# Four rows of a forward substitution as one multiply-add with a column scalar each

## The chip, the cores and the metric

The kernel runs on one core of a Trainium2 chip. Its engines are TensorE (PE, matmuls; PEld is its weight load), VectorE (DVE), ScalarE (ACT), GpSimd (POOL) and SyncE (SP), which here only issues DMAs. The metric is the device time of one execution in microseconds; lower is better. Before the change it is 3082.83 us, the median of three runs (3080.05 to 3083.95).

## The reference

One layer of a hybrid decoder for one sequence of 2048 tokens and 8 short ones of 4, width 1024, 16 heads of 64. A normalised input goes through one wide projection; a short gated convolution and an RWKV-7 recurrence work on parts of it; gates merge the two, an output projection and a residual follow. The part in which the change lies is the recurrence:

```python
def step(S, inp):
    r_t, k_t, v_t, d_t, kk_t, a_t = inp
    sa = jnp.einsum('bhvk,bhk->bhv', S, -kk_t)
    S = (S * d_t[:, :, None, :] + sa[..., None] * (kk_t * a_t)[:, :, None, :]
         + v_t[..., None] * k_t[:, :, None, :])
    y = jnp.einsum('bhvk,bhk->bhv', S, r_t)
    return S, y
```

## The kernel before

**Stages.** The tokens are worked on in four sets of 512 (`th`), and within a set in eight pairs of heads (`p`). While a pair is worked on, TensorE runs projections of the wide matrix for the next pair: blocks of 24 matmuls (8 slices of the contraction, three products of split 32-bit values each), written `ip<-XH,whl` and `ip<-XL,whl` in the profile. `XH` and `XL` are the two parts of the set's input, `whl` the two parts of a weight. After the fourth set come the output projections (`acc`).

**A pair.** The recurrence is computed in chunks of 64 steps: keys (`rwkv_keys`), the solve (`rwkv_solve`), the merge (`rwkv_merge`), loads, the chain over the chunks (`rwkv_chain`: `pa`, `UB`, `pb`, `SV`, `S`), outputs (`rwkv_out`: `Yc`, `mu_`). Each is a generator that yields after a few operations; `drive` runs the projections and lets these side jobs in between.

**The solve.** For each chunk a triangular matrix has to be inverted. Its 32x32 diagonal blocks, two for each of two heads and eight chunks, 32 in all, are inverted by substitution on VectorE. A transpose puts the matrix into `Mi` and the identity into `X` such that a lane holds 8 columns of a block's inverse; then the loop of lines 1215 to 1222 goes over the rows from j = 31 to 1. Row j takes column j of `X` (the 8 - j // 4 column groups that can be other than zero there), multiplies it by row j of `Mi` and adds the product to the columns to the left. These are two operations: the product into `tt`, a buffer of two, and the addition into `X`. For j = 31 to 28 there is one group, number 7, so both have 31 to 28 elements per lane. The 62 operations of a pair depend on each other one by one. Behind them a transpose (`Mi<-X`) makes room for the merge, which runs copies on ScalarE (`Xbd`), transposes on VectorE (`Mc`) and small matmuls (`pt<-Mc`).

**What sets the order.** All engine calls go through one helper (line 264), so that nearly all of the profile's rows are of that line. It books each operation with an assumed cost on a clock of its own: on VectorE 145 ns and 1.05 ns per element, and 58 ns more for a multiply-add with a column scalar (lines 302 to 309). A side job may go on when its inputs are ready by that clock. When all is written down, the instructions of VectorE and ScalarE are put in order of their planned starts and held to it. The order on TensorE, GpSimd and SyncE is that in which the code was written down. So another cost in one operation can move all that follows.

**Splitting weights.** From the second set on, `comb` reads quarters of the output weights (`q`), combines them, and `part_of` splits each into two parts in one of two buffers `qs` by turns and hands a store to `SP.store`. This queue keeps up to two stores back until their data is ready by the planner's clock (lines 324 to 334).

Of the kernel before, what the change touches and what calls it, by code (L numbers as in the profile page):

```python
# [11 lines left out]
ALU = mybir.AluOpType  # L12
# [14 lines left out]
W = {"sq": 1.0, "norm": 1.0, "lora": 2.0, "one": 1.0, "scan": 2.0, "exp": 2.0, "key": 1.0, "bones": 1.5,  # L27
     "sv": 1.5, "bt": 2.0, "score": 4.0, "inv0": 5.0, "inv": 0.45, "inv1": 4.0, "merge": 2.0,
     "gk": 1.3, "us": 1.3, "sa": 1.3, "state": 1.3, "samp": 2.0, "gn": 4.0, "out": 2.0}
# [315 lines left out]
def hybrid_kernel(tc, x_prompt, x_sample, state_conv, state_shift, state_rwkv, norm_g, w_in, conv_w,  # L345
# [5 lines left out]
    V, A, G, T = (Traced(e, n, clock) for e, n in ((nc.vector, "DVE"), (nc.scalar, "ACT"), (nc.gpsimd, "POOL"), (nc.tensor, "PE")))  # L351
    SP = Queue(nc.sync, clock)
# [327 lines left out]
    for q in range(2):  # L680
        V.tensor_tensor(out=mask_s[:, q, 0:NSAMP].rearrange("p (j i) -> p j i", i=SL),
                        in0=mask_p[:, q, 0:NSAMP].rearrange("p (j i) -> p j i", i=SL),
                        in1=seqm.unsqueeze(2).broadcast_to([P, NS, SL]), op=ALU.mult)
# [493 lines left out]
    def rwkv_solve(th, p, o):  # L1177

        AR = o["AR"]
        samp = th == LAST  # L1180
        GM = GMB[(th * NB + p) % 2]


        yield 0.0, (), 2
        for c0 in range(0, NCH + samp, 4):
            cs = range(c0, min(NCH + samp, c0 + 4))
            pp = [new_pt([P, 512], F32, name="pt") for _ in range(2)]
            for c in cs:
                for h in range(2):
                    T.matmul(pp[h][:, (c - c0) * P:(c - c0 + 1) * P], lhsT=BK[HS[h], c].rearrange("p q t -> p (q t)"),  # L1190
                             rhs=AR[HS[h], c].rearrange("p q t -> p (q t)"), start=True, stop=True)
            k = len(cs)
            mk = mask_s if c0 == NCH else mask_p
            for h in range(2):
                V.tensor_tensor(out=GM[:, c0:c0 + k, :, h, :],
                                in0=pp[h][:, 0:k * P].rearrange("p (c a t) -> p c a t", a=2, t=64),
                                in1=mk.unsqueeze(1).broadcast_to([P, k, 2, 64]), op=ALU.mult)
            yield W["score"], (), 2 if c0 + 4 < NCH + samp else 0


        Mc = rw.tile([P, NCH, 32], F32, name="Mc")
        for i, g in enumerate(blk):
            h, b = i // 2, slice(i % 2 * 32, i % 2 * 32 + 32)
            A.copy(Mc[g], GM[b, 0:NCH, 0, h, b])
        yield 0.5, [Mc]
        Mi = rw.tile([P, 32, 32], F32, name="Mi")
        V.transpose(Mi.rearrange("p t (e c) -> p t e c", c=NCH),
                    Mc.rearrange("p c t -> p t c").unsqueeze(2).broadcast_to([P, 32, 4, NCH]))
        X = rw.tile([P, 8, 32], F32, name="X")
        A.copy(X, X0)  # L1210
        Mo = rw.tile([P, NCH, 32], F32, name="Mo")
        A.copy(Mo[64:96], GM[0:32, 0:NCH, 0, 1, 32:64])
        yield W["inv0"], [Mi, X]

        for j in range(31, 0, -1):
            c0 = j // 4
            tt = sm.tile([P, 80], F32, name="tt")
            tv = tt[:, 0:(8 - c0) * j].rearrange("p (c i) -> p c i", i=j)
            V.tensor_tensor(out=tv, in0=Mi[:, j, 0:j].unsqueeze(1).broadcast_to([P, 8 - c0, j]),
                            in1=X[:, c0:8, j:j + 1].broadcast_to([P, 8 - c0, j]), op=ALU.mult)  # L1220
            V.tensor_tensor(out=X[:, c0:8, 0:j], in0=X[:, c0:8, 0:j], in1=tv, op=ALU.add)
            yield W["inv"]
        Xo = rw.tile([P, 32, 32], F32, name="Mi")[:, 0:8].rearrange("p a (e c) -> p a e c", c=8)
        V.transpose(Xo.rearrange("p a e c -> p (a e c)"), X.rearrange("p a b -> p (a b)"))
        o.update(GM=GM, Xo=Xo, Mo=Mo)
        yield W["inv"]
# [333 lines left out]
    def part_of(w, key, j, src, scale=1.0):  # L1560

        hl = qs[turns[0] % 2]
        turns[0] += 1
        yield 1, [src]
        A.activation(out=hl[:, 0], in_=src, func=AF.Copy, scale=scale)
        yield 1, [hl[:, 0]]
        V.scalar_tensor_tensor(out=hl[:, 1], in0=src, scalar=scale, in1=hl[:, 0].bitcast(F32), op0=ALU.mult, op1=ALU.subtract)
        SP.store(units[w][key][j // 2][:, :, j % 2 * 4 * P:(j % 2 + 1) * 4 * P], hl.bitcast(F32))
# [4 lines left out]
    def comb():  # L1573

        add, sub = ALU.add, ALU.subtract
        for w, src in (("c", w_out_c[0]), ("r", w_out_r[0]), ("o", w_o[0])):
            for j in range(4):
# [9 lines left out]
                if w == "o":  # L1587
                    for q in ("11", "12", "21", "22"):
                        yield from part_of(w, q, j, qr[q], 0.5)
                    combined("11", "12", "11", sub)  # L1590
                    yield from part_of(w, "t1", j, qr["11"], 0.5)
                    combined("12", "22", "12", sub)
                    yield from part_of(w, "t3", j, qr["12"], 0.5)
                    combined("22", "22", "11", sub)
                    yield from part_of(w, "t2", j, qr["22"], 0.5)
                    combined("21", "21", "22", sub)
                    yield from part_of(w, "t4", j, qr["21"], 0.5)
                else:
                    for q in ("11", "12", "21", "22") if w == "c" else ("11", "12", "22"):
                        yield from part_of(w, q, j, qr[q])  # L1600
                    combined("22", "21", "22", add)
                    yield from part_of(w, "s1", j, qr["22"])
                    combined("21", "11", "21", sub)
                    yield from part_of(w, "s3", j, qr["21"])
                    combined("22", "22", "11", sub)
                    yield from part_of(w, "s2", j, qr["22"])
                    combined("12", "12", "22", sub)
                    yield from part_of(w, "s4", j, qr["12"])
# [119 lines left out]
    def begin_pair(th, p, total):  # L1728


        o = {}
        k = th * NB + p
        f = [total * x for x in CUTS["end" if end_(th, p) else "most" if th < LAST else "last"]]
        def read(n):
            return [prior(x, n) for x in ("chain", "samp")]
        job["keys", k] = Side(rwkv_keys(th, p, o), "keys", [prior("load", k - 1), prior("solve", k - 1), prior("up", 0)] + read(k - 2)).over(0, f[3])
        job["solve", k] = Side(rwkv_solve(th, p, o), "solve", [job["keys", k], prior("merge", k - 1)] + read(k - 2)).over(f[3], f[4])
        job["merge", k] = Side(rwkv_merge(th, p, o), "merge", [job["solve", k]] + read(k - 2)).over(f[4], f[5])
        job["load", k] = Side(rwkv_load(th, p, o), "load", [job["keys", k]] + read(k - 1)).over(f[4], f[5])
        return o  # L1740
# [389 lines left out]
```

## Time and profile before

| | us |
|---|---|
| median of three runs | 3082.83 |
| the profiled execution | 3081.61 |
| its span in the profile | 3079.9 |
| DVE, products `tt<-Mi,X`, 992 | 216.4 |
| DVE, additions `X<-X,tt`, 992 | 211.0 |

The profile is of one execution. Between its time and the span lie 1.7 us ahead of the first instruction and behind the last. The span is what the engines' rows are measured against. Products and additions of the substitution have 427.4 us together, a fifth of VectorE's busy time. In rows with an instruction, the columns are its start, its duration, the engine, and what it writes and reads; in brackets stands how long the engine was idle before it and what ended that. In grouped rows, the number behind x is the count, then busy time in us and the mean of one in ns. Idle time of an engine that isn't waited for costs nothing.

### The profile page before, as it was taken

What the parts mean: (1) busy time and instruction counts of PE and PEld (TensorE: products, weight loads), DVE (VectorE), ACT (ScalarE), POOL (GpSimd) and SP (SyncE); (2) the same over time, 40 slices, a digit from 0 to 9 for tenths busy, and PEclk for the clock granted to TensorE, in tenths of its full rate; (3) what the DMA queues carried; (4) which work ended last, traced back from release to release, by engine and by line L of the source; (5) the groups of instructions that cost most, each with busy time, mean ns of one, the idle gap of its engine ahead of it and who ended that gap; (6) DMA issues with size and microseconds to landing.
All of it is one profiled execution on the core that took longest, in us unless ns stands there. A gap on an engine that the chain in (4) does not pass through costs nothing. (4 is left out here: it accounts for less than half of the span.)

```text
span 3079.9 us, 56086 instructions
## 1 busy us (share of the span) xinstructions
PE 3004.7 (98%) x21418; PEld 2574.5 (84%) x21418; DVE 2140.3 (69%) x5606; ACT 1338.9 (43%) x2691; POOL 311.2 (10%) x520
## 2 busy tenths in 40 slices
PE   7999999999999999899999999999999999999998
PEld 6777877788878788788888889999999999888996
DVE  5777767766777777777766666666676774486575
ACT  5455555544444444444444444444444442224223
POOL 2011111111111110111111111000000000000000
PEclk9999999999999999999999999999999999999999
DMA  7877767656767676766644444444334447987775
GB/s 270 274 241 239 236 210 255 228 193 222 243 222 235 230 241 218 238 225 239 223 169 155 169 152 151 141 148 144 130 129 144 140 156 239 352 332 291 281 261 193
DMA packets 293937, 659.15 MB, mean 214 GB/s; under 512 B 46394, under 2 KB 162227, under 8 KB 242982
## 3 DMA queue, kind: packets, MB, share of 16 engines
q1 hardware_dynamic: 293670, 655.58, 62.4%
q8 instruction: 169, 2.77, 0.3%
q14 instruction: 98, 0.80, 0.1%
HBM read 472.81 MB, written 182.69 MB: 213 GB/s over the span
## 5 line engine op out<-in xcount | busy, mean ns | idle before, releaser
L264 PE MATMUL ip<-XH,whl 128*128 128x512 f32 (+3 forms) x7088 | 1940.8, 353 | 12.4 <-DVE whl L264 6.4
L264 PEld LDWEIGHTS ip<-XH,whl 128*128 128x128 f32 x7088 | 1223.5, 189 | 156.7 <-DVE whl L264 8.8
L264 PE MATMUL ip<-XL,whl 128*128 128x512 f32 (+3 forms) x3544 | 1248.9, 352 | 2.3 <-POOL XL L264 2.3
L264 PEld LDWEIGHTS ip<-XL,whl 128*128 128x128 f32 x3544 | 671.7, 190 | 73.4 <-issue 5.6
L264 DVE TENSOR_TENSOR tt<-Mi,X 128x60 f32<-128x60 f32 (+24 forms) x992 | 216.4, 218 | 28.6
L264 DVE TENSOR_TENSOR X<-X,tt 128x60 f32<-128x60 f32 (+24 forms) x992 | 211.0, 213 | 31.9
L264 DVE SCALAR_TENSOR_TENSOR S<-pb,pe,sp 64x64 f32<-64x64 f32 x512 | 143.4, 280 | 121.5 <-PE pb L264 114.3
L264 ACT COPY SV<-pb 64x128 f32<-64x128 f32 x256 | 66.0, 258 | 320.6 <-PE pb L264 318.3
L264 ACT ACTIVATE sp<-S,pe 128x128 f32<-128x128 f32 x256 | 102.5, 400 | 227.7 <-DVE S L264 226.8
L264 DVE TENSOR_TENSOR UB<-pa,P 64x64 f32<-64x64 f32 x512 | 110.2, 215 | 124.1 <-PE pa L264 109.5
L264 ACT ACTIVATE tmp<-ip,vec 128x512 f32<-128x512 f32 (+2 forms) x174 | 102.9, 593 | 206.5 <-PE ip L264 200.5
L264 PEld LDWEIGHTS pb<-UB,Xbd 128*128 128x128 f32 x512 | 86.6, 189 | 37.2 <-issue 12.8
L264 ACT COPY Xbd<-Mi 32x256 f32<-32x256 f32 x128 | 88.1, 688 | 62.1 <-DVE Mi L264 60.0
L264 ACT ACTIVATE tmp<-ip 128x512 f32<-128x512 f32 (+2 forms) x126 | 63.0, 500 | 115.2 <-PE ip L264 114.7
L264 DVE TENSOR_TENSOR GM<-pt,mask_p 128x512 f32<-128x512 f32 x128 | 82.4, 686 | 43.8 <-PE pt L264 43.7
L264 PE MATMUL pb<-UB,Xbd 128*128 128x128 f32 x512 | 104.4, 285 | 7.5 <-DVE UB L264 6.7
L264 PEld LDWEIGHTS pb<-SV,BKt 128*128 128x128 f32 x512 | 89.8, 189 | 24.4 <-ACT SV L264 10.0
L264 DVE TENSOR_TENSOR whl<-wraw,whl 128x1024 fp32r<-128x1024 f32 x81 | 103.7, 1280 | 8.7 <-ACT whl L264 8.1
L264 PEld LDWEIGHTS pa<-S,AR 128*128 128x128 f32 x512 | 88.4, 189 | 25.4 <-DVE S L264 12.5
L264 PE MATMUL pb<-SV,BKt 128*128 128x128 f32 x512 | 101.2, 279 | 4.8 <-ACT SV L264 4.8
L264 PE MATMUL pa<-S,AR 128*128 128x128 f32 x512 | 102.3, 281 | 2.6 <-DVE S L264 2.4
L264 PE MATMUL acc<-XL,whl 128*128 128x264 f32 (+1 forms) x616 | 97.9, 309 | 0.0
(554 smaller groups left out, 4325.1 us busy)
## 6 DMA issues: line engine op xcount, KB each, us to landing
wraw<-in_w_in_dram SPq DMA_DIRECT2D x81, 512.0 KB
whl<-w_k SPq DMA_DIRECT2D x24, 1024.0 KB
whl<-w_r SPq DMA_DIRECT2D x24, 1024.0 KB
whl<-w_v SPq DMA_DIRECT2D x24, 1024.0 KB
whl<-w_z SPq DMA_DIRECT2D x24, 1024.0 KB
whl<-w_xin SPq DMA_DIRECT2D x24, 1024.0 KB
whl<-w_cg SPq DMA_DIRECT2D x24, 1024.0 KB
whl<-w_zc SPq DMA_DIRECT2D x24, 1024.0 KB
```

The source lines that it names most:

```text
L264: r = f(*a, **k)
```

## The change

For the first four rows of the substitution, j = 31 to 28, where only column group 7 takes part, product and addition become one operation: row j of `Mi` times a scalar that is column j of `X`, one value per lane, plus `X`, written in place. The other 27 rows stay as they are. The second hunk has `part_of` hand out all stores that are held back before it writes into a buffer that one of them still reads.

```diff
         for j in range(31, 0, -1):
             c0 = j // 4
+            if c0 == 7:
+                V.scalar_tensor_tensor(out=X[:, 7, 0:j], in0=Mi[:, j, 0:j], scalar=X[:, 7, j:j + 1], in1=X[:, 7, 0:j],
+                                       op0=ALU.mult, op1=ALU.add)
+                yield W["inv"]
+                continue
             tt = sm.tile([P, 80], F32, name="tt")
...
         yield 1, [src]
+        if any(x[1].tensor.name == hl.tensor.name for x in SP.due):
+            SP.flush(0)
         A.activation(out=hl[:, 0], in_=src, func=AF.Copy, scale=scale)
```

What it does to the order, first at the start of the first pair's solve on VectorE, as a piece of the difference:

```order
-L264 TENSOR_TENSOR tt<-Mi,X 128x31
-L264 TENSOR_TENSOR X<-X,tt 128x31
-L264 TENSOR_TENSOR tt<-Mi,X 128x30
-L264 TENSOR_TENSOR X<-X,tt 128x30
-L264 TENSOR_TENSOR tt<-Mi,X 128x29
-L264 TENSOR_TENSOR X<-X,tt 128x29
-L264 TENSOR_TENSOR tt<-Mi,X 128x28
-L264 TENSOR_TENSOR X<-X,tt 128x28
+L264 SCALAR_TENSOR_TENSOR X<-Mi,X 128x31
+L264 SCALAR_TENSOR_TENSOR X<-Mi,X 128x30
+L264 SCALAR_TENSOR_TENSOR X<-Mi,X 128x29
+L264 SCALAR_TENSOR_TENSOR X<-Mi,X 128x28
```

Eight operations are replaced by four; this is so in each of the 32 pairs.

Second, VectorE at the change from the second set to the third (1240 to 1275 us of the profile), in the last pair's solve. `rT` is the mixed projection whose reading frees a bank of TensorE's results; the last number of a `tt` row is 8 - j // 4 groups times j. Before:

```order
L264 SCALAR_TENSOR_TENSOR qs_288<-q_284,qs_288 128x512
L264 SCALAR_TENSOR_TENSOR rT<-ip,omu,tmp 128x256
L264 TENSOR_TENSOR tt<-Mi,X 128x54
L264 TENSOR_TENSOR X<-X,tt 128x6x9
L264 TENSOR_TENSOR tt<-Mi,X 128x48
L264 TENSOR_TENSOR X<-X,tt 128x6x8
L264 TENSOR_TENSOR tt<-Mi,X 128x49
```

And of the change:

```order
L264 TENSOR_TENSOR tt<-Mi,X 128x24
L264 TENSOR_TENSOR X<-X,tt 128x8x3
L264 SCALAR_TENSOR_TENSOR rT<-ip,omu,tmp 128x256
L264 TENSOR_TENSOR tt<-Mi,X 128x16
L264 TENSOR_TENSOR X<-X,tt 128x8x2
L264 TENSOR_TENSOR tt<-Mi,X 128x8
L264 TENSOR_TENSOR X<-X,tt 128x8
```

`rT` stood ahead of the solve's last nine rows and stands ahead of its last two.

Third, TensorE at the change from the first set to the second (600 to 670 us). `ip<-ident,wraw` are transposes of the next set's input, `pb` matmuls of the chain. Before:

```order
L264 MATMUL ip<-ident,wraw 128x128 x3
L264 MATMUL pb<-UB_208,Xbd_206 128x128
L264 MATMUL ip<-ident,wraw 128x128
L264 MATMUL ip<-XH,whl 128x256
L264 MATMUL ip<-ident,wraw 128x128 x2
L264 MATMUL pb<-SV,BKt 128x128
L264 MATMUL ip<-ident,wraw 128x128 x2
```

And of the change:

```order
L264 MATMUL pb<-SV,BKt 128x128
L264 MATMUL ip<-ident,wraw 128x128 x4
L264 MATMUL ip<-XL,whl 128x256
L264 MATMUL ip<-XH,whl 128x256
L264 MATMUL ip<-ident,wraw 128x128 x4
L264 MATMUL ip<-XH,whl 128x256
```

The groups of four transposes were cut in two by the chain's matmuls and now stand whole, with the `pb` ahead of them. In all, the instructions on TensorE are the same 17,850 matmuls in another order; VectorE has 5480 rows of instructions where it had 5608.

## The prediction

> **What bounds the kernel.** I read the head of the page first, then the stretches by time, then the waits inside the stretches where TensorE (PE) is not full.
>
> ```profile
> PE 3004.7 (98%) x21418; PEld 2574.5 (84%) x21418; DVE 2140.3 (69%) x5606; ACT 1338.9 (43%) x2691; POOL 311.2 (10%) x520
> 385.00:445.00 60.00, 53.89 (x360) 42.25 (x357) 39.44 (x115) 33.47 (x59) 7.68 (x10) 0.94 0.70 236
> 600.00:670.00 70.00, 61.51 (x525) 55.42 (x523) 58.66 (x152) 29.05 (x63) 9.58 (x14) 0.98 0.64 215
> 670.00:1240.00 570.00, 568.69 (x3799) 462.56 (x3799) 406.98 (x1123) 269.26 (x551) 66.75 (x108) 1.00 0.67 227
> 1240.00:1275.00 35.00, 26.79 (x254) 24.57 (x254) 31.52 (x95) 13.62 (x28) 5.55 (x8) 0.98 0.69 237
> 1845.00:1875.00 30.00, 26.03 (x244) 24.30 (x243) 26.83 (x87) 9.64 (x20) 4.41 (x6) 0.99 0.57 188
> 1875.00:2545.00 670.00, 662.98 (x6023) 624.62 (x6024) 465.12 (x1492) 294.03 (x705) 60.07 (x95) 1.00 0.42 141
> 2666.00:3062.00 396.00, 395.16 (x2340) 349.15 (x2341) 270.70 (x374) 118.97 (x177) 9.80 (x12) 1.00 0.78 283
> ```
>
> The rows are start and end of a stretch, its length, then busy time of PE, weight load, DVE, ACT, POOL, the granted clock and DMA. PE is at work for 98% of the span, and in the long stretches for nearly all of it: 568.69 of 570 and 395.16 of 396 us. There DVE (VectorE) has a quarter to a third of its time free, and a shorter DVE operation can't show. The changes of set are different. In 600 to 670, 1240 to 1275 and 1845 to 1875 DVE is busy for 58.66 of 70, 31.52 of 35 and 26.83 of 30 us, and PE is idle for 8.49, 8.21 and 3.97 us: 20.7 us together. That is where the solve, whose operations the change cuts, can hold PE up. In 385 to 445 PE is idle too, 6.1 us, but DVE is busy for only 39.44 of 60.
>
> What ended the idle time, from the order in time of the first two of these stretches:
>
> ```profile
> 657.83 0.48 DVE L264 SCALAR_TENSOR_TENSOR rT<-ip,omu,tmp 128x256 f32<-128x256 f32 x1
> 658.37 0.51 PE L264 MATMUL ip<-XH,whl 128*128 128x256 f32 x2 [1.54 <-DVE rT L264]
> ...
> 1264.24 0.47 DVE L264 SCALAR_TENSOR_TENSOR rT<-ip,omu,tmp 128x256 f32<-128x256 f32 x1
> 1264.77 0.50 PE L264 MATMUL ip<-XH,whl 128*128 128x256 f32 x2 [0.83 <-DVE rT L264]
> ...
> 1269.83 0.66 PE L264 MATMUL pt<-ident,BK 128*128 128x128 f32 x4 [1.75 <-DVE Yc L264]
> 1272.55 0.21 PE L264 MATMUL pt<-Mc,GM 32*32 32x32 f32 x1 [2.06 <-ACT SV L264]
> ```
>
> PE waits for rT, which stands between rows of the solve in DVE's fixed order, for Yc, which stands behind the solve's end, and for the merge, which needs the solve. All three come earlier by what the solve gets shorter.
>
> **The change: DVE.** Removed are 8 operations per pair, 256 in all; 128 are added. What they take, by group (busy us, mean ns) and in a stretch of the chain with nothing in between:
>
> ```profile
> L264 DVE TENSOR_TENSOR tt<-Mi,X 128x31 f32<-128x31 f32 x32 | 7.8, 245 | 0.8
> L264 DVE TENSOR_TENSOR X<-X,tt 128x31 f32<-128x31 f32 x32 | 6.1, 192 | 1.1
> L264 DVE TENSOR_TENSOR X<-X,tt 128x30 f32<-128x30 f32 x32 | 6.1, 190 | 1.0
> L264 DVE SCALAR_TENSOR_TENSOR cv<-u,cwh,cv 128x32 f32<-128x32 f32 x16 | 4.0, 248 | 0.4
> 2180.47 0.25 DVE L264 SCALAR_TENSOR_TENSOR cv<-u,cwh,cv 128x32 f32<-128x32 f32 x1
> ...
> 2180.75 0.25 DVE L264 SCALAR_TENSOR_TENSOR cv<-u,cwh,cv 128x32 f32<-128x32 f32 x1
> ...
> 2181.67 0.19 DVE L264 TENSOR_TENSOR X<-X,tt 128x30 f32<-128x30 f32 x1
> 2181.89 0.19 DVE L264 TENSOR_TENSOR tt<-Mi,X 128x29 f32<-128x29 f32 x1
> 2182.11 0.19 DVE L264 TENSOR_TENSOR X<-X,tt 128x29 f32<-128x29 f32 x1
> ```
>
> Each operation of the chain starts 0.22 us after the one it depends on (2181.67, 2181.89, 2182.11), so a row of the substitution takes 0.44 us. (The 245 of the first product I leave aside: what follows it is at 190 to 192.) The new form does not occur on X, but its like does: the convolution's taps are product and addition in place, 128x32, with a column scalar, and the second starts 0.28 us after the first that it depends on. I take 0.28; the saving is 0.16 us per row, 0.64 us per pair, and 128 x 0.16 = 20.5 us of DVE's 2140.3. The ends: 0.22 if the scalar costs nothing (0.88 us per pair), 0.44 if a scalar written just before costs as much as a second operation (nothing saved).
>
> The scalar is a column that the row before has just written. The nearest case is in the last stage:
>
> ```profile
> 3065.37 0.41 DVE L264 SCALAR_TENSOR_TENSOR f<-f,f 128x1 f32<-128x1 f32 x2 [0.66 <-POOL f L264]
> 3065.82 0.75 DVE L264 SCALAR_TENSOR_TENSOR Rx<-Rx,f,fg 128x512 f32<-128x512 f32 x1
> ```
>
> f is done at 3065.78, and the operation that takes it as scalar starts 0.04 us later, as after a tensor operand; so I add nothing for it. [...]
>
> **What of it is on the path.** The planner counts a shorter solve and places the merge's matmuls earlier, so in the long stretches PE only finds other work in another order: 0. In the three DVE-bound stretches one solve each runs: 3 x 0.64 = **1.9 us less**, at most 2.6, and nothing if rT and the transposes are placed worse by as much.
>
> **What it moves.** The planner places everything anew. The stream of projections on PE is cut into by other matmuls 1273 times where it was 1257 times (counted over the two built orders; 17,850 matmuls in both). What a cut costs:
>
> ```profile
> 2172.64 0.38 PE L264 MATMUL pa<-S,AR 128*128 128x128 f32 x2
> 2172.78 0.38 PE L264 MATMUL ip<-XH,whl 128*128 128x288 f32 x1
> 2173.00 0.29 PE L264 MATMUL ip<-XL,whl 128*128 128x288 f32 x1
> 2173.12 0.43 PE L264 MATMUL ip<-XH,whl 128*128 128x288 f32 x2
> ```
>
> From start to start a projection of this form takes 0.12 us (2173.00 to 2173.12), the one just behind the cut 0.22: 0.10 lost, 16 x 0.10 = **1.6 us more**. The ends are 0 and, by the weight loads in front of the small matmuls (pt) that stood for 32.9 us in 98 cases, 0.34 each, 16 x 0.34 = 5.4.
>
> ```profile
> PEld pt L264 <- issue: 32.9, 98, 1.2
> ```
>  In 600 to 670 the cuts get fewer: the transposes for the next set, cut apart by the state loop's matmuls (pb) in the old order, stand as whole groups of four in the new.
>
> The second hunk holds once in the new build: one store of a split weight (uc, from qs) goes out ahead of a weight load (whl from w_k) instead of behind it, and SP's queue, which runs in order, waits for DVE's qs there before it issues that load and what follows.
>
> ```profile
> SPq L337 <- DVE qs L264: 221.5, 76, 7.2
> 1172.75 0.56 SPq L337 DMA_DIRECT2D whl<-w_xin  x1
> ...
> 1201.58 0.32 SPq L337 DMA_DIRECT2D whl<-w_gc  x1
> ```
>
> SP waits for qs 76 times already, 2.9 us on average, 7.2 at most. Between the load for xin and that for gc, four blocks on, lie 28.8 us, 7.2 us per block, and weights are asked for up to three blocks ahead: cover for some 20 us, less the transfer. I cost it at nothing; without the cover it would be those 2.9 to 7.2 us, once.
>
> The sum against the profiled execution (3081.61, span 3079.9): -1.9 + 1.6 = -0.3, so 3081.3; the median of the three runs shown is 1.2 above that execution. I forecast **3081 us**, no change that a measurement can tell: about 0.2%, or 6 us, is what one of this kernel resolves, and the cases below go by that bound.
>
> **Rivals.**
>
> (a) The new order falls well. PE's idle time at the four uneven places above sums to 26.8 us (20.7 + 6.1). It is not owed to work but to the order: the same change of set costs 8.5, 8.2 and 4.0 us. If the first two became like the third, 8.8 us would go on top of the forecast's sum. That gives **3072.5**. For it: DVE is the last releaser there and has 20 us less to do; the whole groups of transposes. Against it: the planner goes by the same costs as before, and nothing in it aims at these stretches.
>
> (b) Slower: rT is placed behind the solve. PE's next projection needs the bank that rT frees. At 1264.24 nine rows of the solve stand behind rT, in the new order two. Seven rows of 0.44 are 3.1 us more wait at that place, if DVE is as late there as it was. The same can befall kT, the lora operands and the transposes' inputs; the two worst stretches cost about 8.5 us of idle each, and doubling one is 8.5 us, which gives **3090**. It decides from the point at which rT ends later on DVE than PE takes to reach its next projection, which in the old trace it did by 0.83 and 1.54 us. Against it: the solve is 0.64 us shorter, the scaled inputs (wraw) are spread over more rows, and in 600 to 670 rT stands behind the same row in both orders.
>
> (c) The change doesn't do what it says: a column scalar costs 0.22 us more than a plain operation. Then DVE's time stays, the 1.9 go, and only the cuts remain: 3083.
>
> **How the numbers follow.** The bounds of 0.2% lie at 3077 and 3089, around the median of before. My forecast with (c) gets 0.42; (a) 0.34; (b) 0.24. As nothing in the trace ties the re-placed waits to one sign, (a) gets more for DVE's 20 us alone. The predicted time is the likeliest case's own. The range leaves one in ten at each side: down past (a) to 3066, since the two worst stretches' 16.7 us of idle time could go almost wholly, up past (b) to 3095, one stretch doubled and the cuts at their upper end. The forecast's own range is 3077 to 3087, its sum with the ends of both terms and some 4 us of re-placed waits. Chances: faster 0.34, the same 0.42, slower 0.24.
>
> **What would show it.** DVE with 128 operations and about 20 us less busy time; the new group on X at about 248 ns, with starts 0.28 us apart; tt and X as product and addition 864 times each, where they were 992. PE's idle time in the three stretches near 20 us. The forecast is wrong if that idle time is below 12 or above 28 us, if SP's wait for qs has one well over 7.2 us followed by an idle PE, or if the new operation is nearer to 0.44 than to 0.28.

## The result, and the profile after

| | median us | ratio to before, 95% interval |
|---|---|---|
| before | 3082.82 (3080.05 to 3085.85, 6 runs) | |
| changed | 3055.57 (3055.01 to 3058.84, 6 runs) | 0.9913 [0.9903, 0.9923] |

The change makes the kernel 27 us faster, 0.87%, where 3081 was forecast. The profiled execution took 3055.37, its span is 3053.7, 26.2 less than before.

First the head of the page and, from the view of the cores, span and granted clock of before and of after:

```profile
PE 2990.0 (98%) x21418; PEld 2566.6 (84%) x21418; DVE 2127.0 (70%) x5478; ACT 1339.7 (44%) x2691; POOL 317.3 (10%) x520
core 0: 3079.9 us, clock 0.995
core 0: 3053.7 us, clock 0.997
```

The 26.2 us split in three. TensorE's idle time is 75.2 us before (3079.9 - 3004.7) and 63.7 after: 11.5 less. The granted clock took 0.005 x 3079.9 = 15.4 us before and 0.003 x 3053.7 = 9.2 after: some 6 less, an estimate from rounded clocks. The rest, some 8 us, is gone from time in which TensorE counts as busy.

Where it went, by the same work in both traces (stretches between the same finished projections, to within half a microsecond; columns as in the prediction's windows). Before:

```profile
377.50:509.90 132.40, 125.20 (x762) 99.32 (x761) 97.91 (x268) 63.94 (x117) 15.24 (x24) 0.97 0.72 240
581.90:669.80 87.90, 79.41 (x667) 69.76 (x665) 70.82 (x178) 44.51 (x88) 14.34 (x19) 0.98 0.63 212
2105.50:2235.60 130.10, 129.02 (x1183) 121.43 (x1179) 87.10 (x294) 60.41 (x142) 12.09 (x19) 1.00 0.43 143
```

After:

```profile
378.90:502.60 123.70, 120.47 (x747) 95.63 (x747) 95.72 (x259) 67.21 (x123) 15.30 (x24) 1.00 0.78 246
576.20:657.80 81.60, 76.97 (x604) 68.21 (x602) 65.50 (x160) 38.60 (x78) 13.25 (x15) 0.98 0.69 237
2088.10:2212.60 124.50, 123.45 (x1152) 117.75 (x1150) 83.61 (x276) 58.99 (x137) 12.03 (x19) 1.00 0.46 152
592.00:658.80 66.80, 62.44 (x531) 56.53 (x531) 56.47 (x141) 28.92 (x60) 10.00 (x14) 0.97 0.67 233
1225.50:1258.80 33.30, 27.59 (x257) 25.27 (x256) 29.22 (x91) 14.20 (x28) 5.81 (x8) 0.97 0.77 263
1827.50:1857.10 29.60, 25.74 (x245) 24.05 (x243) 26.57 (x84) 9.88 (x21) 4.50 (x6) 1.00 0.57 191
```

The first three rows pair with those of before: 132.4 to 123.7, 87.9 to 81.6 and 130.1 to 124.5 us, some 21 of the 26. Other stretches gain or lose less. The last three rows are the prediction's changes of set: idle time there (length less PE) is 4.36, 5.71 and 3.86, together 13.9 us where it was 20.7. The edges matter: when each stretch is cut behind the last projection that had ended in before's, it is 11.5. The largest piece lies where the prediction had set a stretch aside, another where TensorE had counted as busy for 129 of 130 us.

The new operation itself, by group:

```profile
L264 DVE SCALAR_TENSOR_TENSOR X<-Mi,X 128x31 f32<-128x31 f32 x32 | 9.2, 289 | 1.0
L264 DVE SCALAR_TENSOR_TENSOR X<-Mi,X 128x30 f32<-128x30 f32 x32 | 8.0, 249 | 1.0
```

It takes 249 ns in the row of 30 elements and 267 in the mean of all 128, and the next row starts 0.285 us after it (median of the trace), where product and addition took 0.45 together.

### The profile page after: what moved, and what is told of

Read it like the earlier page. It is cut to its first block, busy times and chain, and to the rows that moved or that the text cites. A ratio compares the mean times of both kernels' runs of the same rounds, so it can differ in the third digit from the quotient of the medians.

```text
span 3053.7 us, 55957 instructions
## 1 busy us (share of the span) xinstructions
PE 2990.0 (98%) x21418; PEld 2566.6 (84%) x21418; DVE 2127.0 (70%) x5478; ACT 1339.7 (44%) x2691; POOL 317.3 (10%) x520
## 5 line engine op out<-in xcount | busy, mean ns | idle before, releaser
L264 DVE TENSOR_TENSOR X<-X,tt 128x60 f32<-128x60 f32 (+21 forms) x864 | 188.1, 218 | 27.8
L264 DVE TENSOR_TENSOR tt<-Mi,X 128x60 f32<-128x60 f32 (+21 forms) x864 | 188.8, 219 | 25.2
```

What stands on the lines that cost most here:

```text
L264: r = f(*a, **k)
```

## The experiments

Before's 3083 us is the yardstick on every chip; each ratio is to runs of before beside it, and 0.1% is 3.1 us. The time of one kernel varies with the granted clock: the first kernel below ran between 3073.3 (clock 0.997) and 3083.7 (0.994). An order of the instructions that the planner happens to make, one of many that it could as well have made, is called a draw.

**Operation and order apart.** The planner can be told one thing and the engines given another. `book` puts a cost on the planner's clock and issues nothing; what is issued while `clock.at` is set takes that planned start. For the rows j = 31 to 28 (`row` is row j of `Mi`, `c` column j of `X`, `x` the columns to its left), first the old operations in the changed kernel's order:

```diff
+                clock.at = V.book("scalar_tensor_tensor", x, row, c, x, scalar=c)
+                V.tensor_tensor(out=tt[:, 0:j], in0=row, in1=c.broadcast_to([P, j]), op=ALU.mult)
+                V.tensor_tensor(out=x, in0=x, in1=tt[:, 0:j], op=ALU.add)
+                clock.at = None
```

> Product and addition as before in all 31 rows, but the planner is told the cost of one multiply-add for the rows j = 31 to 28, so that the engines' orders are the changed kernel's (29 of 17,852 rows of TensorE stand elsewhere, of ScalarE none). Theory ORDER (the 27 us come from the re-placed instructions, not from VectorE's shorter work): 3056 to 3062, the gain stays. Theory OPERATION (the shorter solve is what counts): 3078 to 3084. VectorE's busy time as before, near 2140.

And the new operation in the order of before:

```diff
+                V.book("tensor_tensor", tt[:, 0:j], row, c)
+                clock.at = V.book("tensor_tensor", x, x, tt[:, 0:j])
+                V.scalar_tensor_tensor(out=x, in0=row, scalar=c, in1=x, op0=ALU.mult, op1=ALU.add)
+                clock.at = None
```

> The changed kernel's one operation for j = 31 to 28, but the planner is told the cost of product and addition, so that the orders are those of before (26 of 17,852 rows of TensorE stand elsewhere). ORDER: 3077 to 3083, at most the 1.9 to 2.6 us of the three changes of set are gained. OPERATION: 3056 to 3062. The 2.9 us gap of TensorE near 390 us should be there by ORDER and gone by OPERATION.

Then the four rows left out in either order: the bookings stay, the instructions go.

> Leaves out the rows j = 31 to 28 of the substitution altogether (the inverse is then not the reference's); the planner is told that they are there, so the orders are those of before. VectorE has about 1.8 us less per pair than before, where the kernel with one operation in the old order has 0.66 less and took 0.33% off. Theory CHAIN (TensorE's chain matmuls wait for UB and S, which stand on VectorE among the rows of the solve, in all stretches): more than with one operation, up to the 1.8/0.66 of it, 3055 to 3068, and the excess of the steps from a projection to a small matmul falls below 87 us. Theory PLACES (only single stalls near 390, 417 and at the changes of set gain): within 3 us of 3070.

> Leaves out the rows j = 31 to 28 (the inverse is then not the reference's) with the planner told of the one operation, so the orders are the changed kernel's (5 of 17,852 rows of TensorE stand elsewhere). VectorE has 4 x 0.285 = 1.14 us less per pair than the changed kernel, 36 us in all. Theory CHAIN, at the 0.4 us of time per us of VectorE that the two runs in the old order gave: 14 us off, 3038 to 3045. If the changed kernel's order leaves the chain nothing to wait for: within 3 us of 3055.

Measured, as ratios to before:

| rows j = 31 to 28 | order of before | order of the changed kernel |
|---|---|---|
| product and addition | 1 | 0.9984 [0.9973, 0.9994] |
| one operation | 0.9967 [0.9954, 0.9979] | 0.9913 [0.9903, 0.9923] |
| left out | 0.9918 [0.9903, 0.9933] | 0.9866 [0.9851, 0.9881] |

(The middle right cell is the changed kernel.) Neither ORDER nor OPERATION holds alone: 3078.87 us fits OPERATION, 3070.46 lies between the two theories' ranges. In the order of before, the operation gives 10 us; the new order without it gives 5; both give 27. The gap near 390 us is still there with the operation in the old order, at 1.94 us. Going down a column, VectorE's time buys time: in the order of before 10 us for 20.8 us of VectorE (0.65 per pair, rows below) and 25 for 57.3 (1.79 per pair), in the changed kernel's order 14 more for 36. That is 0.4 to 0.5 us per us. Both runs without the rows lie in CHAIN's ranges (3058.57 and 3042.10 us), and not in PLACES'. (From product and addition to the one operation in the changed kernel's order it is more, 22 for 20.8.)

How it can, where TensorE is busy, is seen in the second set, in the chain of its third pair. Before, on VectorE (the first and last of the eight operations, the last row ahead of `UB`, then `UB`) and on TensorE:

```profile
944.37 0.19 DVE L264 TENSOR_TENSOR tt<-Mi,X 128x31 f32<-128x31 f32 x1
...
945.94 0.19 DVE L264 TENSOR_TENSOR X<-X,tt 128x28 f32<-128x28 f32 x1
946.16 0.22 DVE L264 TENSOR_TENSOR tt<-Mi,X 128x54 f32<-128x54 f32 x1
...
948.14 0.45 DVE L264 TENSOR_TENSOR UB<-pa,P 64x64 f32<-64x64 f32 x2
944.69 0.38 PE L264 MATMUL pa<-S,AR 128*128 128x128 f32 x2
...
947.70 0.40 PE L264 MATMUL ip<-XL,whl 128*128 128x512 f32 x1
947.93 0.63 PE L264 MATMUL ip<-XH,whl 128*128 128x512 f32 x2
948.40 0.39 PE L264 MATMUL ip<-XL,whl 128*128 128x512 f32 x1
948.73 0.46 PE L264 MATMUL pb<-UB,Xbd 128*128 128x128 f32 x2
```

The same place with the new operation in the same order:

```profile
935.31 1.10 DVE L264 SCALAR_TENSOR_TENSOR X<-Mi,X 128x31 f32<-128x31 f32 x4
936.45 0.22 DVE L264 TENSOR_TENSOR tt<-Mi,X 128x54 f32<-128x54 f32 x1
...
938.42 0.45 DVE L264 TENSOR_TENSOR UB<-pa,P 64x64 f32<-64x64 f32 x2
935.63 0.38 PE L264 MATMUL pa<-S,AR 128*128 128x128 f32 x2
...
939.34 0.39 PE L264 MATMUL ip<-XL,whl 128*128 128x512 f32 x1
939.56 0.38 PE L264 MATMUL pb<-UB,Xbd 128*128 128x128 f32 x2
```

`UB` needs `pa`, done at 945.07, and stands on VectorE behind eight rows of the solve; it is done at 948.59. `pb` starts 0.33 us after the projection ahead of it, where the same projection is otherwise followed in 0.23 (947.70 to 947.93). These 0.10 us are a wait, but the projection's row of 0.39 ends at 948.79, behind the start of `pb`, so that no idle time is booked: the ends of matmuls are modelled in the profile. With the four rows in 1.14 us instead of 1.79, `UB` is done 0.69 us ahead of `pb`, which follows in 0.22.

Worked out over the trace, outside of stretches with the clock down: the time from the end of `pa` to the start of `UB` is 1.13 us in the mean of 256 chunks before, 1.07 with the operation and 0.97 with the rows left out, all in one order; the step into `pb<-UB` falls from 200 to 187 and 182 ns, that into `pa<-S` from 178 to 174 and 174. With some 510 steps of each, the operation saves 6.6 + 2.0 us there.

The sum over all matmuls of the chain (`pa`, and `pb` from `UB` and from `SV`; each step from the start of the matmul ahead, half of the time at half clock taken off, an estimate of what that costs) tells the same, and whatever the order. In the seven traces of orders with product and addition that this document has, it is 276.5 to 289.7 us, 282.4 in the mean; in the seven with the one operation 269.8 to 273.7, 272.6 in the mean. The two don't overlap, and they lie 10 us apart. Between before and the operation in the old order it falls by 9.4 us, steps into the merge's matmuls (`pt<-Mc`) by 2.5 and into transposes of the next input by 1.2, of 12.9 us between the two spans. With the rows left out in the old order the chain's share is 12.2 of 23.1 us; the merge has 4.0 of the rest, projections 4.6, other small matmuls 2.8. So the chain is most of what the operation gives, and half of what leaving the rows out gives.

Where the wait is long enough to be booked, the view of TensorE's waits (total us, count, longest) has it, here for before, the operation in the old order, the rows left out in the old order, the old operations in the new order, and after:

```profile
PE pb L264 <- DVE UB L264: 6.7, 12, 1.2
PE pb L264 <- DVE UB L264: 3.1, 7, 1.2
PE pb L264 <- DVE UB L264: 1.9, 5, 0.6
PE pb L264 <- DVE UB L264: 12.0, 19, 1.3
PE pb L264 <- DVE UB L264: 4.5, 11, 0.9
```

The fourth row fits with the new order giving so little without the operation: planned for rows of 0.27 us, it gets rows of 0.45, and `UB` comes late at 19 places.

**The stall near 390 us.** Before, ScalarE's squares of the next input (`tmp<-wraw`) stand ahead of an `SV` copy and wait 1.92 and 1.99 us for their loads, and TensorE waits for `SV`:

```profile
388.18 1.06 ACT L264 ACTIVATE tmp<-wraw 128x1024 bf16<-128x1024 f32 x1 [1.92 <-DMA wraw<-in_x_prompt_dram]
391.32 1.06 ACT L264 ACTIVATE tmp<-wraw 128x1024 bf16<-128x1024 f32 x1 [1.99 <-DMA wraw<-in_x_prompt_dram]
392.38 0.24 ACT L264 COPY SV<-pb 64x128 f32<-64x128 f32 x1
392.67 0.69 PE L264 MATMUL pb<-SV,BKt 128*128 128x128 f32 x2 [2.89 <-ACT SV L264]
```

In the changed kernel this gap is 0.47 us. To see what it is worth alone, the loads' booked latency is raised, in the kernel before and in the changed one:

```diff
-            SP.dma_start(out=xt, in_=x_prompt[0, i * P:(i + 1) * P, :])
+            SP.dma_start(out=xt, in_=x_prompt[0, i * P:(i + 1) * P, :], lag=6000.0)
...
-        SP.dma_start(out=xt[s * NS:(s + 1) * NS], in_=xs_v[s])
+        SP.dma_start(out=xt[s * NS:(s + 1) * NS], in_=xs_v[s], lag=6000.0)
```

> The kernel before with the second hunk's guard, and the loads of the later sets' input booked at 6 us of latency where it was 2 (the other loads as before). The orders are the same up to about 340 us; then ScalarE's squares of the input (tmp<-wraw), which waited 1.9 and 2.0 us for their loads near 390 us, stand behind the SV copies for which TensorE waited 2.9 us. Theory STALL (that place is a matter of the order alone): idle time and lost clock in 378 to 510 us fall by 4 to 8 us, and about as much of the whole, 3075 to 3079. Theory DRAW (what is gained there is given back where the order is then another): within 3 us of 3083.

> The changed kernel with the input loads of the later sets booked at 6 us of latency; the orders are the changed kernel's up to about 340 us. In the kernel before, this edit removed the 2.9 us gap near 390 us and gave as much back behind it. Theory DRAW: 3053 to 3070, no better than the changed kernel. If a truer latency is of use by itself: under 3053.

Measured: 0.9997 [0.9988, 1.0006] and 0.9932 [0.992, 0.9945]. In the first, the gap is gone. Its rows for the work of before's 377.5 to 509.9 us and of the stretch behind it (before: 132.4 and 71.9 us):

```profile
380.40:509.30 128.90, 123.75 (x761) 98.14 (x761) 95.24 (x252) 64.92 (x120) 11.72 (x22) 0.99 0.75 240
509.30:582.00 72.70, 70.76 (x465) 55.53 (x464) 56.40 (x161) 36.98 (x70) 9.00 (x13) 1.00 0.73 232
...
842.82 1.00 PE L264 MATMUL pt<-ident,tmp 128*128 128x128 f32 x4 [2.69 <-ACT tmp L264]
```

3.5 us are gained there, a little under STALL's 4 to 8, and 0.8 given back at once. (That as much is given back right behind the place, as the second expectation has it, isn't so between the same projections.) What undoes the rest lies elsewhere: this trace has lost 2.9 us before the stretch begins (its granted clock is 0.993 over the whole span, where before's is 0.995), and it loses 3.6 between 800 and 1000 us, where the last row shows a gap of 2.69 us that before does not have. As a whole the kernel is no faster: DRAW, and not STALL. It is one order; what filling the gap gives with all else the same isn't shown.

**By sets.** The operation in the first set's pairs alone, and in the others alone:

```diff
-            if c0 == 7:
+            if c0 == 7 and th == 0:
```

> The changed kernel with the one operation in the first set's eight pairs alone; the other 24 pairs have product and addition. The orders are the changed kernel's up to the end of the first set and a new draw behind it. If the gain of the first 600 us (7 to 11 us in the changed kernel's trace) stays and nothing else does: 3072 to 3076. If the later sets need the shorter operation for what they gained: no more than that. If another draw falls as well without it: down to 3060.

> The changed kernel with product and addition in the first set, and the one operation in the 24 pairs of the later sets; the orders are those of before to the end of the first set. Theory CHAIN: the first 600 us as before, then some 0.3 us per pair, 7 us, with a draw of 5 us on either side: 3070 to 3081. If the first set held all of the gain: 3080 to 3084.

Measured: 0.9961 [0.9949, 0.9974] and 0.9953 [0.994, 0.9965]. In the trace of the first, 14.1 us are gained by 670 us and 12.5 at the end; in that of the second 0.9 are lost by then and 13.6 gained at the end. The two sum to the changed kernel's 0.87%: about half is earned up to the first change of set, the other half behind it. Both came out better than expected (3070.19 against 3072 to 3076, 3067.91 against 3070 to 3081), and each has a draw of its own in it: the chain's sum falls by 6.5 and 3.8 us.

**Other orders.** What remains is the order. The same instructions are placed anew by booking VectorE at 143 to 147 ns and its length instead of 145, or the multiply-add 75 ns dearer instead of 58, as it was measured:

```diff
-            return 145 + per * n + 58 * one
+            return 144 + per * n + 58 * one
```

> The kernel before with every VectorE operation booked at 144 ns and its length instead of 145, and the second hunk's guard for the buffer: same instructions, another order. ORDER: the time is a new draw, several us off 3083 on either side (up to 25), following TensorE's idle time and clock in 375 to 455 us. OPERATION: within 3 us of 3083, as nothing is shorter.

> As the kernel with 144, with 146 ns: another draw. ORDER: several us off 3083 on either side (up to 25). OPERATION: within 3 us of 3083.

> The changed kernel with every VectorE operation booked at 146 ns and its length instead of 145: same instructions, another order. If the changed kernel's own order is a lucky draw: 3060 to 3070, what the operation gives by itself with an ordinary order. If the shorter solve gives its whole gain in any order: 3053 to 3059.

> The changed kernel with a multiply-add with a column scalar booked 75 ns above a plain operation instead of 58, so that a row's start-to-start time in the plan is the 0.285 us measured. Another order. Theory DRAW (an order's worth is scattered by 5 to 10 us whatever is booked): 3058 to 3072. Theory TRUE COST (a plan with true times gives a better order): 3055 or less.

> The kernel before with the guard, VectorE booked at 143 ns and its length. Another order with product and addition. If such orders scatter around -0.2% with 0.2% on either side: 3070 to 3083. If the order of before is ordinary and the two at -0.34 and -0.46% were lucky: 3080 to 3090.

> As the kernel with 143, with 147 ns. Around -0.2%: 3070 to 3083. Ordinary order of before: 3080 to 3090.

> The changed kernel with VectorE booked at 143 ns and its length. Another order with the one operation. If such orders scatter around -0.75% with 0.2% on either side: 3053 to 3066. If the operation gives 0.33% and the rest is luck: 3066 to 3076.

> As the changed kernel with 143, with 147 ns. Around -0.75%: 3053 to 3066. Operation 0.33% and luck: 3066 to 3076.

| booked | product and addition | one operation |
|---|---|---|
| 143 | 1.0018 [1.0009, 1.0027] | 0.9934 [0.9921, 0.9948] |
| 144 | 0.9966 [0.9954, 0.9979] | |
| 145 | 1 (before) | 0.9913 [0.9903, 0.9923] (changed) |
| 146 | 0.9954 [0.994, 0.9968] | 0.9949 [0.9936, 0.9961] |
| 147 | 0.9966 [0.9953, 0.9978] | 0.9987 [0.9977, 0.9997] |
| 145 and 75 | | 0.9908 [0.9894, 0.9921] |
| late loads | 0.9997 [0.9988, 1.0006] | 0.9932 [0.992, 0.9945] |

Worked out from the six of each column: the means are -0.17% and -0.63%, and single orders scatter by 0.25 and 0.29% (standard deviation). So one nanosecond in a booking moves the time by 4 to 16 us, on either side. The means differ by 0.46%, 14 us, with a standard error of 0.16%, 5 us; the chain's 10 us lie within one such error of it. The order of before is 5 us worse than the mean of its column, the changed kernel's 7 us better than that of its own. The expectation that plans with the one operation stay between 3053 and 3066 failed with 147 ns, 3078.82. Of the plans with product and addition, 143 ns gave 3089.09, as if the order of before were ordinary, and 147 ns 3073.24, as if it were a poor one: each expectation came true once. True costs gave 3052.9, a ratio that can't be told from the changed kernel's.

## Why the prediction was wrong

- **The step that failed** is "in the long stretches PE only finds other work in another order: 0". In the order of before, the operation alone gave 10 us, against 1.9 forecast; of the 12.9 us between the two traces, 9.4 are shorter steps into the chain's matmuls. The reading behind it was wrong: "568.69 of 570" does not say that TensorE waits for nothing, as modelled ends cover waits of 0.1 us. In 12, 11 and 11 of the 64 chunks of the first three sets (in none of the fourth) rows of the solve are still to run on VectorE when `pa` is done, ahead of the chain's `UB`, and a shorter row lets `UB` start earlier.
- **The three changes of set** were about right in themselves: with the orders of before, the operation took 1.0 + 2.2 + 0.3 us of TensorE's time there with the clock's loss left aside, where 1.9 was forecast, at most 2.6. In the changed kernel 6.8 us of idle time went. The sign that was to show the forecast wrong (idle time there under 12 us) is at 13.9 or 11.5, as the stretches are cut, so it was no clear sign: it watched the wrong places.
- **The clock** has no term in the sum. By the records, 15.8 us were lost to half clock before and 9.2 in the changed kernel's trace, 6.6 less; as the clock differs between executions (0.990 to 0.996 over the runs of before beside the others, 0.996 and 0.997 over six of the changed kernel), part of it is luck.
- **"385 to 445 is set aside"** as not bound by VectorE. The largest piece of the result lies there, 8.7 us. With the operation in the old order the same stretch is 4.5 us shorter, 3.4 of them clock. But the run with late loads, in which the gap is filled, was no faster as a whole.
- **The re-placed waits** were given some 4 us on either side of the forecast, and 8.8 in rival (a). Orders scatter by about 8 us, and the changed kernel's is a good one beside a poor one of before: about 12 of its 27 us, by the means of six, are luck. Rival (a) was right in sign and had a third of the chance; its 3072.5 lies 9 us above the mean of the orders with the one operation, 0.9937 or 3063.
- **The operation's cost** was right: 249 ns in the rows of 30 elements, a start 0.285 us later, nothing added for the fresh column; rival (c) is out. "About 20 us less busy time" was mis-sized: 13.3 on the page, as busy time counts durations and not the gaps between them (tt and X were 427.4 us and with the new group are 411.1).
- **The cuts**, 1.6 us more, can't be seen. They came as counted, 1273 for 1257. The old operations in the new order have as many, and TensorE's busy time at full clock is 5 us less there than before, not more.
- **Rival (b)**, rT behind the solve, did not come: at that change of set TensorE's wait for rT is 0.53 us where it was 0.83, and the idle time fell from 8.21 to 5.71 us.
- **The second hunk**, costed at nothing: SP's waits for `qs` are 77 with 7.8 us the longest (76 and 7.2 before), so the sign "well over 7.2" did not show. What the hunk costs by itself no run tells.

```profile
SPq L337 <- DVE qs L264: 214.9, 77, 7.8
```

What the other 16 to 17 us between the operation in the old order and the changed kernel consist of can be told in part. The two traces' spans are 13.4 us apart, and of these the chain has 0.4: it gains nothing by the new order. 6.8 us are half clock, 4.9 shorter steps into projections, 2.5 into other small matmuls; the transposes of the next input lose 1.8. 2.3 us of the small matmuls' share can be read in the stretch 2105 to 2235, of whose 5.6 us the old operations in the new order gain 4.8 as well. There stand 36 `pt<-AR,BK`, of which here is one row of before and one of the changed kernel:

```profile
2163.71 1.75 PE L264 MATMUL pt<-AR,BK 64*128 64x128 f32 x12
2144.76 1.16 PE L264 MATMUL pt<-AR,BK 64*128 64x128 f32 x16
```

Before, most of them start one by one, 0.11 us apart; in the changed kernel's order they start in pairs, 7 ns apart. The mean step into one falls from 139 to 76 ns, 2.3 us for the 36; with the operation in the old order the row of 1.75 us is the same, and with the old operations in the new order 16 take 1.16. So it is a matter of the order; why some start in pairs and others don't is left open, and so is the rest of that stretch. How much of the new order's gain a plan for short rows earns, and how much is the draw, the means alone tell, with 5 us either way. All kernels with product and addition here share the order's rules; whether other rules scatter as much was not tried.

## What to carry to other kernels

Where a fixed order is planned from booked costs, a change of one cost is two changes: run the new operation in the old order and the old in the new before crediting either, and take a few neighbouring bookings, since one order's worth scatters by as much as many a change brings (here by 0.25 to 0.29%). An engine that is "busy" for 99% can still wait in many steps, as TensorE did here (568.69 of 570 us, and a step into `pb<-UB` of 0.33 us where 0.22 were enough): compare start-to-start times of the same instruction with and without a dependent one behind it. Where an engine's order is fixed, an operation that stands ahead of the one that the bottleneck waits for can be on the path, as the solve's rows ahead of `UB` were here, and leaving it out tells at once what the rest is worth (25 us in the order of before, where the operation gave 10).

## What was not expected of the hardware

In some stretches the granted clock is 0.50. Before's clock records have six of 3.41 us, one of 6.83 and one that runs past the end of the span; the changed kernel's have four of 3.41 and one at the end. Each 3.41 us cost 1.7, an estimate: half of their length. (From start to start a projection of 128x512 takes 427 ns in them and 233 at full clock, the median in either trace; by that it would be 1.55.) Two of before's stand behind gaps of TensorE of 2.89 and 2.06 us (the latter ahead of a projection at 419.33), one of the changed kernel's behind a gap of 1.56:

```profile
392.80:396.20 3.40, 3.40 (x11) 2.82 (x12) 0.57 (x2) 3.30 (x8) 0.00 (x0) 0.50 1.02 387
420.10:423.50 3.40, 3.40 (x9) 2.65 (x8) 3.28 (x9) 0.00 (x0) 0.00 (x0) 0.50 0.88 272
1854.99 0.24 PE L264 MATMUL pt<-Mc,GM 32*32 32x32 f32 x2 [1.56 <-DVE Yc L264]
1857.80:1861.10 3.30, 3.30 (x16) 3.30 (x15) 1.84 (x6) 2.38 (x5) 0.83 (x1) 0.50 0.00 0
```

A gap does not settle it. Ahead of the two stretches at the ends of the spans there is none in the last 5 us; ahead of the others the longest is 0.51 to 2.89 us (0.51 ahead of before's at 2249.7). And behind before's gap of 2.24 at 609.3 the clock stays full (1.00 from 609.3 to 619). The granted clock differs between executions of one kernel, and by the estimate that is most of their spread: from clock 0.997 to 0.994 an estimate of 9 us, of the 10 between the fastest and the slowest run of the old operations in the new order.
